# Row totals of two output norms by VectorE blocks of 32, and the second norm's factors as a row by HBM

## The chip, the cores and the metric

The kernel runs on one core of a Trainium2 chip. It computes one layer of an encoder block in float32. The metric is the device time of one execution in microseconds (us). Each engine (TensorE or PE for matmuls, VectorE or DVE, ScalarE or ACT, GpSimd or POOL, SyncE or SP for transfers) runs its own list of instructions in order, and semaphores tie the lists together.

## The reference

There are 256 tokens (S) of width 2048 (D). Cut to what matters here, with every norm an RMS norm (divide by the root of the mean square, multiply by a gain):

```python
h = rmsnorm(x, norm1_g)
q, k, v, u = split(h @ w_in)
a = rmsnorm(window_attention(q, k, v, sink), attn_out_g)   # 1536 wide: AW
f = rmsnorm(fourier_mix(u, w_fourier), fourier_out_g)      # 512 wide: FW
x = x + concatenate([a, f]) @ w_out
h = rmsnorm(x, norm2_g)
up = h @ w_up                                # gate (5504 wide) | value (5504 wide)
gate = depthwise_conv3(up_gate) + dw_b
x = x + (gelu(gate) * up_value) @ w_down
return rmsnorm(x, normf_g)
```

The change concerns three factors per token: those of the norms of `a` and of `f`, which are applied after the output projection, and that of the norm before `w_up` (the second norm), which is applied to the results of the up-projection.

## The kernel before, in words

**Products.** A float32 operand is split into a rounded half `hi` and the rest `lo`, and a product is three matmuls (hi·hi, lo·hi, hi·lo). The weights come from HBM as units of 128x2048 (1 MB, tile `raw`, three buffers), SP issuing the loads (L165). ACT writes `hi` (L181), DVE writes `lo` (L182); each has three buffers, so the split of a unit waits until PE is done with the unit three before it. The list of units, in order: 0 to 3 for u, 4 to 7 for v, 8 to 23 for the heads of k and q (32 matmuls each, L350), 24 to 39 for the output projection (24 matmuls each, L333 to L335), then one unit for each gate tile and each value tile of the up-projection (units 40, 41, 42, ... ; L350), mixed with the down-projection.

**The order of work.** It is written out by hand. `unit(i, work)` runs for each unit i: the list `before[i]`, the matmuls, the list `beside[i]`, then `step(i)`, which splits unit i + 2 and so issues the load of unit i + 5, then `behind[i]`. `at(when, i, f, ...)` puts f in one of these lists. In the up-projection `ff_step(n)` does the same for item n (item 0 is the first gate tile, item 1 the first value tile, and so on; item n is unit 40 + n here). `N_OUT` is 24.

**Sums for `a` and `f`.** The heads and Fourier groups are held with features on partitions and the 256 tokens along the free side. POOL adds up their squares into `sq_f` and `sq_a` (128 partitions x 256 tokens, L490). A token's total is thus a sum over partitions. `total` (L494) forms it on PE: two float32 matmuls with a column of `ones`, into a bank of `ps_tot`, at the head of unit 14 for `f` and of unit 30 for `a`. `total_scale` calls `rstd_of` (L274): DVE multiplies and adds EPS (L277), POOL raises to the power -0.5 (L280). The result `r_af[part]`, 128x2, holds tokens on partitions. `out_add` (L808) applies it on DVE when a result of the output projection leaves PSUM (L811); the first use for `f` is beside unit 29, for `a` behind unit 30.

**The second norm.** ACT sums the squares of the new x by rows (L285, `ssq2`). After the first two up-projection items have been multiplied in pieces (the pair: chunks 0 to 11 of item 0, `ff_step(0)`, the transposes of the last quarter of x on PE in `turn_x(3)`, chunks 0 to 11 of item 1, then chunks 12 to 15 of both), DVE reduces `ssq2` (L1225), `rstd_of` makes the factors with tokens on partitions, and `spread` (L289) turns them into a row that stands on all partitions: two diagonal matrices on DVE (L294), two float32 matmuls with `ones` on PE (L297), a copy on DVE out of PSUM into `r2b` (L300). Every up-projection result is then multiplied by `r2b` in `scaled_sum` (L920 to L925): ACT copies one half of the bank, DVE adds the other half (this frees the PSUM bank), DVE multiplies by `r2b`.

**A row by HBM.** `row_by_hbm` (L304) makes such a row without PE: a transfer from POOL's queue writes the 256 factors to HBM one by one (L307), a second reads them back as a row on all 128 partitions (L308). Before the change it is used once, for the first norm (`r1b`, behind unit 4).

**PSUM.** Up-projection results use the four banks of `mm` in turn, so item n needs the bank of item n - 4. `spread`, `total`, scores, values and transposes share the four banks of `dn`. `up_posts(n, ...)` puts `scaled_sum` beside item n + 1, the convolution of a gate tile beside and its GELU behind n + 2, and the product of gate and value beside n + 2.

Of the kernel before, what the change touches and what calls it, by code (L numbers as in the profile page):

```python
# [8 lines left out]
F32 = mybir.dt.float32  # L9
# [95 lines left out]
def block_kernel(  # L105
# [30 lines left out]
    def bank(pool, name):  # L136
        return pool.tile([P, 512], F32, tag=pool.name, name=name)
# [114 lines left out]

    ones = base.tile([P, P], F32, tag="ones", name="ones")
    nc.gpsimd.memset(ones, 1.0)
    half_pow = base.tile([P, 2], F32, tag="half_pow", name="half_pow")
    nc.gpsimd.memset(half_pow, -0.5)
    ident = base.tile([P, P], F32, tag="ident", name="ident")
    make_identity(nc, ident)
# [15 lines left out]
    def rstd_of(ssq, width, name, n=2, r=None):  # L274

        var = base.tile([P, n], F32, tag="var" + name, name="var" + name)
        nc.vector.tensor_scalar(var, ssq, 1.0 / width, EPS, ALU.mult, ALU.add)  # L277
        if r is None:
            r = base.tile([P, n], F32, tag="rstd" + name, name="rstd" + name)
        nc.gpsimd.tensor_tensor(r, var, half_pow[:, 0:n], ALU.pow)  # L280
        return r

    def row_ssq(parts, t, c, b, name):
# [1 line left out]
        nc.scalar.activation(  # L285
            junk, t[:, b, :], AF.Square, accum_out=parts[:, b, c : c + 1]
        )

    def spread(r, dst, name):  # L289

        t = wp.tile([P, 512], F32, tag="junk", name=f"diag{name}")
        dgs = [t[:, b * P : (b + 1) * P] for b in range(2)]
        for b, dg in enumerate(dgs):
            nc.vector.tensor_scalar(dg, ident, r[:, b : b + 1], None, ALU.mult)  # L294
        ps = bank(dn, "ps_spread" + name)
        for b in range(2):
            nc.tensor.matmul(  # L297
                ps[:, b * P : (b + 1) * P], ones, dgs[b], start=True, stop=True
            )
        nc.vector.tensor_copy(dst, ps[:, :S])  # L300

    rows = ctx.enter_context(tc.tile_pool(name="rows", bufs=1, space=bass.MemoryType.DRAM))

# [71 lines left out]
    def at(when, i, f, *a):  # L375
        when.setdefault(i, []).append((f, a))
# [112 lines left out]
        if not first:  # L489
            nc.gpsimd.tensor_tensor(sq, sq, one, ALU.add)  # L490

    sums, r_af = {}, {}

    def total(sq, part):  # L494
        ps = bank(dn, "ps_tot" + part)
        for b in range(2):
            nc.tensor.matmul(
                ps[:, b : b + 1], sq[:, b * P : (b + 1) * P], ones[:, 0:1],
                start=True, stop=True,
            )  # L500
        sums[part] = ps

    def total_scale(part, width):
        r_af[part] = rstd_of(sums.pop(part)[:, 0:2], width, part)


    held = {}
# [98 lines left out]
    def fourier_channels_steps():  # L606
        for g in range(NG):
            i = 8 + g
            at(before, i, fourier_channels, g)
            at(beside, i, fourier_channels_copy, g)  # L610
            at(behind, i, fourier_channels_join, g)
            at(beside, i + 1, fourier_channels_out, g)
        at(before, 14, total, sq_f, "f")
        at(beside, 14, total_scale, "f", FW)


    ps_v = [bank(mm, f"ps_v{b}") for b in range(2)]
# [206 lines left out]
    def turn_x(c):  # L824
        turn_x_out(c, turn_x_in(c))
# [47 lines left out]
                )  # L873
        hT2.append(t)

    at(before, N_OUT + 6, total, sq_a, "a")
    at(beside, N_OUT + 6, total_scale, "a", AW)
    ps_a = {}
    for n, (c, kq) in enumerate(OUT_ORDER):
        i = N_OUT + n  # L880
# [188 lines left out]
    def ff_step(n):  # L1069
        todo, later[:] = list(later), []  # L1070
        for f in todo:
            next(f, None)
        run(beside, n)
        split_item(n + 2)
        for f in todo:
            for _ in f:
                pass
        run(behind, n)

    def up_posts(n, kind, j, ps):  # L1080
        if kind == "gate":
            at(beside, n + 1, scaled_sum, ps, f"g{j}")
            at(beside, n + 2, gate_conv, j)
            at(behind, n + 2, gate_gelu, j)
        else:
            at(beside, n + 1, scaled_sum, ps, f"v{j}")
            at(beside, n + 2, val_mult, j)
            if j + 1 in [first + 2 * n for first, n in GROUPS]:
                g = group_of(j)[0]
                at(behind, n + 1, operand, g, "P1")  # L1090
                at(behind, n + 2, operand, g, "N4")
                at(behind, n + 3, operand_sums, g, 0)
# [120 lines left out]
    for q in range(2):  # L1213
        kind, j = items[q]
        ps = bank(mm, f"ps_{kind}{j}")
        pair.append((ps, *halves.pop(n_front + q)))
        still_weights(*pair[q][1:], ps, range(12))
        if q == 0:
            ff_step(0)
            turn_x(3)  # L1220
            hT[:] = hT2
    for ps, hi, lo in pair:
        still_weights(hi, lo, ps, range(12, NK))
    tot2 = base.tile([P, 2], F32, tag="tot2", name="tot2")
    nc.vector.tensor_reduce(tot2, ssq2, mybir.AxisListType.X, ALU.add)  # L1225
    spread(rstd_of(tot2, D, "2"), r2b, "2")
    ff_step(1)
    up_posts(1, *items[0], pair[0][0])
    up_posts(2, *items[1], pair[1][0])

    for n, it in enumerate(items):
        if n < 2:
# [205 lines left out]
```

## Time and profile before

| what | us |
|---|---|
| median of the runs shown | 938.24 (938.22 to 939.98, 3 runs) |
| the profiled execution's own time | 937.84 |
| its span, first to last instruction | 936.1 |
| PE busy in it | 926.8 |
| DVE busy | 767.0 |
| ACT busy | 541.3 |
| POOL busy | 62.2 |

The profile is one execution. The span leaves out what lies around the first and the last instruction, 1.74 us here. Matmuls are pipelined, so one of them overlaps the next; what a group of matmuls costs is the distance from the end of the group before it to its own end, and this is how the chain of waits counts. Times in the text are microseconds from the start of the span.

### The profile page before, as it was taken

To read this page: it belongs to the slowest core of one execution; us is meant where nothing else is said; L and a number is where in the kernel's file an instruction comes from. 1 tells how busy PE (TensorE), PEld (TensorE's weight loads), DVE (VectorE), ACT (ScalarE), POOL (GpSimd) and SP (SyncE) were. 2 spreads that over 40 slices of the span, in tenths; PEclk is the share of its full clock that TensorE was granted. 3 is DMA by queue.
4 is the path that set the end of the run, shared out by engine and by line. 5 is a ranking of instruction groups with operands and counts; after the bars stand their busy time and mean duration, and the time that the engine had idled before them with its cause. 6 is when DMAs were issued, how large, how long until landed. Compare 5 with 4: busy or idle time off the path is not lost.

```text
span 936.1 us, 12843 instructions
## 1 busy us (share of the span) xinstructions
PE 926.8 (99%) x5005; PEld 802.8 (86%) x5005; DVE 767.0 (82%) x958; ACT 541.3 (58%) x672; POOL 62.2 (7%) x80
## 2 busy tenths in 40 slices
PE   9999999999999999999999999999999999999996
PEld 7889998888888888888888888888888888888885
DVE  7668988577677887798877997878979789989986
ACT  6756777545464646566555665555655556655553
POOL 0101211100000000000000000000000000000002
PEclk9999999999999999999999999999999999999999
DMA  9965777567766568788797778777787968779652
GB/s 360 319 223 163 244 236 209 185 206 264 249 226 220 187 203 263 254 270 259 222 293 257 235 217 291 232 260 234 260 247 241 307 223 270 242 230 275 197 180 90
DMA packets 55149, 223.26 MB, mean 239 GB/s; under 512 B 21136, under 2 KB 25744, under 8 KB 31536
## 3 DMA queue, kind: packets, MB, share of 16 engines
q1 hardware_dynamic: 50544, 192.94, 57.1%
q0 software_dynamic: 4544, 29.49, 16.6%
q8 instruction: 39, 0.64, 0.3%
q14 instruction: 22, 0.18, 0.1%
HBM read 216.13 MB, written 6.29 MB: 238 GB/s over the span
## 4 chain that ended last, share of the span: by engine, by line
PE 98%; DVE 1%; DMA 0%; ACT 0%; issue 0%; DVEq 0%; POOLq 0%; POOL 0%; ACTq 0%
PE ps_val L350 25%; PE ps_gate L350 25%; PE ps_q L350 7%; PE ps_P L1149 3%; PE ps_P L1147 3%; PE ps_P L1148 3%; PE ps_N L1149 3%; PE ps_N L1147 3%; PE ps_N L1148 3%; PE ps_a L335 2%; PE ps_k L350 2%; PE ps_a L333 2%; PE ps_a L334 2%; PE ps_s L657 1%; PE ps_o L751 1%; PE ps_ff L333 1%
## 5 line engine op out<-in xcount | busy, mean ns | idle before, releaser
L182 DVE TENSOR_TENSOR lo<-raw,hi 128x2048 fp32r<-128x2048 f32 (+1 forms) x129 | 293.4, 2274 | 40.4 <-ACT hi L181 40.0
L181 ACT ACTIVATE hi<-raw 128x2048 fp32r<-128x2048 f32 (+1 forms) x129 | 245.5, 1903 | 36.9 <-PE ps_a L334 14.9
L350 PE MATMUL ps_val<-hU,hi 128*128 128x512 f32 x688 | 236.2, 390 | 0.0
L350 PE MATMUL ps_gate<-hU,hi 128*128 128x512 f32 x688 | 236.2, 390 | 0.0
L350 PE MATMUL ps_val<-hU,lo 128*128 128x256 f32 x688 | 190.3, 277 | 0.0
L350 PE MATMUL ps_gate<-hU,lo 128*128 128x256 f32 x688 | 190.3, 277 | 0.0
L350 PEld LDWEIGHTS ps_gate<-hU,hi 128*128 128x128 f32 x688 | 129.2, 188 | 26.8
L350 PEld LDWEIGHTS ps_val<-hU,hi 128*128 128x128 f32 x688 | 129.2, 188 | 26.8
L350 PEld LDWEIGHTS ps_gate<-hU,lo 128*128 128x128 f32 x688 | 129.3, 188 | 1.3
L350 PEld LDWEIGHTS ps_val<-hU,lo 128*128 128x128 f32 x688 | 129.3, 188 | 1.3
L922 ACT ACTIVATE ft_g<-ps_gate 128x256 f32<-128x256 f32 x43 | 16.5, 384 | 123.0 <-PE ps_gate L350 123.0
L922 ACT ACTIVATE ft_v<-ps_val 128x256 f32<-128x256 f32 x43 | 16.5, 384 | 91.7 <-PE ps_val L350 91.7
L350 PE MATMUL ps_q<-hT,hi 128*128 128x512 f32 x192 | 65.1, 392 | 0.0
L1147 PE MATMUL ps_P<-hi_P,op_P 128*128 128x512 f32 x144 | 56.1, 390 | 0.0
L1149 PE MATMUL ps_P<-lo_P,op_P 128*128 128x512 f32 x144 | 56.1, 390 | 0.0
L1148 PE MATMUL ps_P<-hi_P,op_P 128*128 128x512 f32 x144 | 56.1, 389 | 0.0
L350 PE MATMUL ps_q<-hT,lo 128*128 128x256 f32 x192 | 51.3, 277 | 0.0
L1039 DVE TENSOR_TENSOR lo_N<-sumw,hi_N 128x2048 fp32r<-128x2048 f32 (+1 forms) x20 | 41.5, 2076 | 9.4 <-ACT hi_N L1038 9.2
L1147 PE MATMUL ps_N<-hi_N,op_N 128*128 128x512 f32 x108 | 42.1, 390 | 0.0
L1148 PE MATMUL ps_N<-hi_N,op_N 128*128 128x512 f32 x108 | 42.1, 390 | 0.0
L1149 PE MATMUL ps_N<-lo_N,op_N 128*128 128x512 f32 x108 | 42.1, 390 | 0.0
L350 PEld LDWEIGHTS ps_q<-hT,hi 128*128 128x128 f32 x192 | 35.3, 188 | 6.5
(390 smaller groups left out, 1589.9 us busy)
## 6 DMA issues: line engine op xcount, KB each, us to landing
raw<-in_w_up SPq DMA_DIRECT2D x86, 1024.0 KB, 5.7
raw<-in_w_in SPq DMA_DIRECT2D x20, 1024.0 KB, 6.5
raw<-in_w_out SPq DMA_DIRECT2D x16, 1024.0 KB, 4.9
sumw<-in_w_down POOLq DMA_DIRECT2D x16, 1024.0 KB, 8.4
raw<-in_w_down_late SPq DMA_DIRECT2D x4, 1024.0 KB, 7.0
raw<-in_w_down_last SPq DMA_DIRECT2D x4, 768.0 KB, 4.1
turnp<-flip SPq DMA_DIRECT2D x40, 64.0 KB, 1.9
flop<-turnp SPq DMA_DIRECT2D x10, 256.0 KB, 3.5
```

Source lines behind the costliest of these rows:

```text
L181: nc.scalar.activation(hi[:, 0:n], raw[:, 0:n], AF.Copy)
L182: nc.vector.tensor_tensor(lo[:, 0:n], raw[:, 0:n], f32(hi[:, 0:n]), ALU.subtract)
L333: nc.tensor.matmul(ps, ah, wh, start=first and q == q0, stop=False)
L334: nc.tensor.matmul(ps, al, wh, start=False, stop=False)
L335: nc.tensor.matmul(ps, ah, wl, start=False, stop=last and q == q0 + len(kk) - 1)
L350: nc.tensor.matmul(ps[:, x], (hi, lo)[i][:, k * P : (k + 1) * P], hk(k)[:, x], start=n == 0 and k == 0, stop=n == len(order) - 1 and k == ...
L657: nc.tensor.matmul(ps[:, b * S : (b + 1) * S], qT[:, qo + b * P : qo + (b + 1) * P], kT[:, ko : ko + S], start=n == 0, stop=n == 2,)
L922: nc.scalar.activation(tmp, ps[:, S : 2 * S], AF.Copy)
L1039: nc.vector.tensor_tensor(lo, src, f32(hi), ALU.subtract)
L1147: nc.tensor.matmul(ps, o[:, 0, p, :], hi[:, s], start=first and p == 0, stop=False)
L1148: nc.tensor.matmul(ps, o[:, 1, p, :], hi[:, s], start=False, stop=False)
L1149: nc.tensor.matmul(ps, o[:, 0, p, :], lo[:, s], start=False, stop=last and p == n - 1)
```

## The change

`total` and `spread` go. `total_scale` now takes the sums of squares themselves and does all on DVE but the power: it transposes the 128x256 tile in blocks of 32x32, so that in each block the 32 partitions' values of a token lie side by side, adds them up (one reduction to 128x8), brings the three lower quarters of partitions next to the first (three copies of 32x8), adds the four, scales, lets POOL raise 32x8 to the power, and puts the result on 128x2 by four copies of 32x2. The calls move: for `f` from unit 14 to behind unit 25 (after the split of unit 27), for `a` from unit 30 to behind unit 29 (after the split of unit 31).

The factors of the second norm are formed right after `ff_step(0)`, ahead of `turn_x(3)`, and go to `r2b` by `row_by_hbm`. The work behind items 0 and 1 moves one item later (`up_posts` with 2 and 3 in place of 1 and 2).

```diff
-    half_pow = base.tile([P, 2], F32, tag="half_pow", name="half_pow")
+    half_pow = base.tile([P, 8], F32, tag="half_pow", name="half_pow")
...
-    def spread(r, dst, name):
...
-    def total(sq, part):
-        ps = bank(dn, "ps_tot" + part)
-        for b in range(2):
-            nc.tensor.matmul(
-                ps[:, b : b + 1], sq[:, b * P : (b + 1) * P], ones[:, 0:1],
-                start=True, stop=True,
-            )
-        sums[part] = ps
-
-    def total_scale(part, width):
-        r_af[part] = rstd_of(sums.pop(part)[:, 0:2], width, part)
+    def total_scale(sq, part, width):
+
+        t = ph.tile([P, S], F32, tag="tmp", name=f"turned_{part}", bufs=2)
+        nc.vector.transpose(t, sq)
+        w = ph.tile([P, S], F32, tag="add", name=f"sums_{part}", bufs=2)
+        q = w[:, 0:32].rearrange("p (q f) -> p q f", q=4)
+        nc.vector.tensor_reduce(
+            q[:, 0, :], t.rearrange("p (f i) -> p f i", f=8), mybir.AxisListType.X, ALU.add
+        )
+        for k in range(1, 4):
+            nc.vector.tensor_copy(q[0:32, k, :], q[32 * k : 32 * (k + 1), 0, :])
+        tot = base.tile([P, 8], F32, tag="var" + part, name="var" + part)[0:32]
+        r = w[0:32, 32:40]
+        nc.vector.tensor_reduce(
+            tot, q[0:32].rearrange("p q f -> p f q"), mybir.AxisListType.X, ALU.add
+        )
+        nc.vector.tensor_scalar(tot, tot, 1.0 / width, EPS, ALU.mult, ALU.add)
+        nc.gpsimd.tensor_tensor(r, tot, half_pow[0:32], ALU.pow)
+        d = r_af[part] = base.tile([P, 2], F32, tag="rstd" + part, name="rstd" + part)
+        by_block = r.rearrange("p (b f) -> p f b", b=2)
+        for k in range(4):
+            nc.vector.tensor_copy(d[32 * k : 32 * (k + 1)], by_block[:, k, :])
...
-        at(before, 14, total, sq_f, "f")
-        at(beside, 14, total_scale, "f", FW)
+        at(behind, N_OUT + 1, total_scale, sq_f, "f", FW)
...
-    at(before, N_OUT + 6, total, sq_a, "a")
-    at(beside, N_OUT + 6, total_scale, "a", AW)
+    at(behind, N_OUT + 5, total_scale, sq_a, "a", AW)
...
             ff_step(0)
+            tot2 = base.tile([P, 2], F32, tag="tot2", name="tot2")
+            nc.vector.tensor_reduce(tot2, ssq2, mybir.AxisListType.X, ALU.add)
+            row_by_hbm(rstd_of(tot2, D, "2"), r2b, "2")
             turn_x(3)
...
-    tot2 = base.tile([P, 2], F32, tag="tot2", name="tot2")
-    nc.vector.tensor_reduce(tot2, ssq2, mybir.AxisListType.X, ALU.add)
-    spread(rstd_of(tot2, D, "2"), r2b, "2")
     ff_step(1)
-    up_posts(1, *items[0], pair[0][0])
-    up_posts(2, *items[1], pair[1][0])
+    up_posts(2, *items[0], pair[0][0])
+    up_posts(3, *items[1], pair[1][0])
```

More of the change, by code (lines that the diff above doesn't have):

```diff
@@ L287, in row_ssq @@
         )
-    def spread(r, dst, name):
[L291 to L295, printed above, removed]
-        for b in range(2):
-            nc.tensor.matmul(
-                ps[:, b * P : (b + 1) * P], ones, dgs[b], start=True, stop=True
-            )
-        nc.vector.tensor_copy(dst, ps[:, :S])
     rows = ctx.enter_context(tc.tile_pool(name="rows", bufs=1, space=bass.MemoryType.DRAM))
@@ L490, in feature_out @@
             nc.gpsimd.tensor_tensor(sq, sq, one, ALU.add)
-    sums, r_af = {}, {}
-    def total(sq, part):
-        ps = bank(dn, "ps_tot" + part)
-        for b in range(2):
-            nc.tensor.matmul(
-                ps[:, b : b + 1], sq[:, b * P : (b + 1) * P], ones[:, 0:1],
-                start=True, stop=True,
-            )
-        sums[part] = ps
-    def total_scale(part, width):
-        r_af[part] = rstd_of(sums.pop(part)[:, 0:2], width, part)
+    r_af = {}
+    def total_scale(sq, part, width):
[19 more added lines that the diff above has]
+            nc.vector.tensor_copy(d[32 * k : 32 * (k + 1)], by_block[:, k, :])
     held = {}
```

## The prediction

> **What bounds the kernel now.** I read the page first (busy times, shares of the chain), then the chain in order of time around the three places that the change touches, then the transfers, and last the instructions of POOL, DVE and ACT around those places.
>
> ```profile
> PE 926.8 (99%) x5005; PEld 802.8 (86%) x5005; DVE 767.0 (82%) x958; ACT 541.3 (58%) x672; POOL 62.2 (7%) x80
> PE 98%; DVE 1%; DMA 0%; ACT 0%; issue 0%; DVEq 0%; POOLq 0%; POOL 0%; ACTq 0%
> ```
>
> PE is busy for 926.8 us of a span of 936.1, and 98% of the chain that ended last is PE itself. So a microsecond taken out of PE's list is a microsecond of the kernel, wherever it stands, and work on DVE, ACT, POOL or the queues costs nothing as long as it does not make PE wait. The whole question is then how much leaves PE, and whether one of the new detours is long enough to stop it.
>
> The chain shows the three pieces of PE work that go. Columns: start, length, what, number of instructions.
>
> ```profile
> 84.70 5.48 PE ps_q L350 x32
> 90.18 0.34 PE ps_totf L497 x4
> 90.51 5.58 PE ps_q L350 x32
> 183.17 0.23 PE ps_ff L333
> 194.11 0.34 PE ps_tota L497 x4
> 194.45 0.34 PE ps_ff L333
> 195.94 0.23 PE ps_ff L333
> 260.81 0.44 PE ps_spread L297 x4
> 261.25 5.45 PE ps_gate L350 x32
> 277.58 5.44 PE ps_val L350 x32
> ```
>
> **Part 1, PE's own work.** The reader sees 0.34 us for the total of `f`, 0.34 for that of `a`, 0.44 for `spread`, and that the work behind each is a little longer than its like: 5.58 against 5.48 us for a unit of 32 matmuls (0.10), 0.34 against 0.23 for the first matmul behind the total of `a` (0.11), 5.45 against 5.44 behind `spread` (0.01). Removed: 0.34 + 0.10 + 0.34 + 0.11 + 0.44 + 0.01 = 1.34 us. If the small excesses have another cause, it is 0.34 + 0.34 + 0.44 = 1.12. I take 1.34, because the excess stands directly behind the removed group in two cases of three.
>
> **Part 2, the totals on DVE.** These are the rows of DVE around the new places of the two calls.
>
> ```profile
> 157.93 0.71 DVE L314 STREAM_TRANSPOSE flip<-sc 128x512 f32<-128x512 f32 x1
> 165.25 2.29 DVE L182 TENSOR_TENSOR lo<-raw,hi 128x2048 fp32r<-128x2048 f32 x1
> 172.34 2.29 DVE L182 TENSOR_TENSOR lo<-raw,hi 128x2048 fp32r<-128x2048 f32 x1 [0.48 <-ACT hi L181]
> 190.43 2.29 DVE L182 TENSOR_TENSOR lo<-raw,hi 128x2048 fp32r<-128x2048 f32 x1 [0.44 <-ACT hi L181]
> 195.86 2.29 DVE L182 TENSOR_TENSOR lo<-raw,hi 128x2048 fp32r<-128x2048 f32 x1 [1.22 <-ACT hi L181]
> ```
>
> And these are POOL's powers and its two transfers for the row of the first norm, then DVE's and ACT's rows around the second norm.
>
> ```profile
> 35.73 2.71 POOL L280 TENSOR_TENSOR rstd<-var,half_pow 128x2 f32<-128x2 f32 x1 [34.25 <-DVE var L277]
> 38.77 0.93 POOL L307 DMA_DIRECT2D row<-rstd  x1 [0.32 <-POOL rstd L280]
> 49.48 0.59 POOL L308 DMA_DIRECT2D r1b<-row  x1 [9.78 <-DMA row<-rstd]
> 257.37 0.69 POOL L280 TENSOR_TENSOR rstd<-var,half_pow 128x2 f32<-128x2 f32 x1 [61.95 <-DVE var L277]
> ```
>
> ```profile
> 250.76 2.29 DVE L182 TENSOR_TENSOR lo<-raw,hi 128x2048 fp32r<-128x2048 f32 x1 [0.18 <-ACT hi L181]
> 254.09 0.48 DVE L270 SCALAR_TENSOR_TENSOR hU<-ps_x,vec,hU 128x256 fp32r<-128x256 f32 x1 [1.04 <-ACT hU L269]
> 256.94 0.15 DVE L1225 TENSOR_REDUCE tot<-ssq 128x2 f32<-128x8 f32 x1
> 257.12 0.17 DVE L277 TENSOR_SCALAR var<-tot 128x2 f32<-128x2 f32 x1
> 263.83 0.42 DVE L924 TENSOR_TENSOR fa_g<-ps_gate,ft_g 128x256 f32<-128x256 f32 x1
> 264.28 0.43 DVE L925 TENSOR_TENSOR fa_g<-fa_g,r2b 128x256 f32<-128x256 f32 x1
> 264.62 2.29 DVE L182 TENSOR_TENSOR lo<-raw,hi 128x2048 fp32r<-128x2048 f32 x1
> 266.82 0.48 DVE L933 SCALAR_TENSOR_TENSOR cv<-fa_g,vec,cv 128x255 f32<-128x255 f32 x1
> 267.74 0.41 DVE L924 TENSOR_TENSOR fa_v<-ps_val,ft_v 128x256 f32<-128x256 f32 x1
> ```
>
> ```profile
> 251.91 0.19 ACT L285 ACTIVATION_READ_ACCUMULATOR junkb<-xs 128x1 f32 x1
> ```
>
> One call of the new `total_scale` costs DVE a transpose of half the size of the one shown, between 0.35 and 0.71 us, say 0.45; a reduction over 256 elements, for which no row exists, taken like the 256-element operations at 0.42 to 0.48; nine small operations like the 0.15 and 0.17 of the reduction and scaling, 9 x 0.16 = 1.4; and the wait for POOL's power, 0.69 and some 0.1 of handing over. That is 3.1 us, an estimate from these rows. The power has been seen at 0.69 and at 2.71; the 2.71 lies over a run of DVE's split, and here DVE waits idle, so I take 0.69; with 2.71 the call takes 5.1. In front of `f` stands the split of unit 27 (165.25, ends 167.54), so the call ends at about 170.6. Even if all 3.1 or 5.1 us went into the next split (172.34, ends 174.63), unit 28 would be ready at 177.7 or 179.7, and PE opens it at 183.17. For `a` the call runs from 192.72 to about 195.8, in a gap in which DVE waits anyway until 195.86; with 5.1 us the next split, of unit 32, ends at 200.1 and PE opens unit 32 two units of some 5.4 behind the one at 194.45, at 205.3. Cost 0 at the value taken and at the upper end; the cover is a lead of 5 us or more, and what a call took beyond it would be PE's. The factor for `a` is first used behind unit 30, after that split, as before.
>
> **Part 3, the row by HBM.** Reduction and scaling move from 256.94 to the end of the split at 250.76, that is 253.05 (ACT's last sum of squares has ended at 252.10); they take 0.18 + 0.17 of the 1.04 us in which DVE then waits for ACT, so the transposed x is not later. POOL's list is empty there. Its power starts 0.25 behind the scaling, as at 257.37, at 253.48 and ends at 254.17; the write of the 256 factors is issued 0.33 later, 254.50. For the two transfers there is one precedent, and two neighbours (size, median to landing):
>
> ```profile
> turnp<-flip SPq DMA_DIRECT2D x40, 64.0 KB, 1.9
> gfb<-in_normf_g POOLq DMA_DIRECT2D x1, 1024.0 KB, 4.5
> r1b<-row POOLq DMA_DIRECT2D x1, 128.0 KB, 6.9
> row<-rstd POOLq DMA_DIRECT2D x1, 1.0 KB, 10.1
> ```
>
> At least, a write to HBM lands in 1.9 us and a broadcast in 4.5; the precedent says 10.1 and 6.9. I take the precedent, since it is the same pair of instructions: row landed at 264.6, read issued 0.6 later (48.87 to 49.48 in the precedent) at 265.2, `r2b` landed at X = 272.1. The lower end is 254.50 + 1.9 + 0.6 + 4.5 = 261.5.
>
> Who waits for X? DVE, in the first multiplication by `r2b`, which now stands beside item 3, behind the splits of items 3 and 4; DVE would be there near 265.5, so it stands still for up to 6.6 us. Behind it on DVE, by the rows at 264.28 to 267.74: the rest of that multiplication 0.34, addition and multiplication for item 2 0.45 + 0.34, the split of item 5 2.20, the convolution 0.92, and then the addition that frees the PSUM bank of item 1, 0.41. Together X + 4.66 = 276.8. PE needs that bank for item 5, which begins at 277.58 now and 0.45 earlier without `spread`, 277.13 (the 0.89 of the two totals moves everything here alike). So there are 0.35 us to spare, and a landing later than 272.5 makes PE wait by as much as it is later. The next in line, the split of item 6, would be ready about 4.2 us later, at X + 8.9 = 281.0, against 283.02 - 0.45 = 282.57 of PE. The bank of item 0, needed for item 4, is freed by an addition that stands ahead of the wait. Cost taken: 0.
>
> The Trainium skill, "DMA: Bandwidth & Descriptors", section "Anatomy of one DMA — SWDGE (gpsimd) path", puts such a transfer at about 2.0 us fixed plus its bytes over the bandwidth, most of the fixed part being the receipt of the write, and calls the delay long where the target is HBM. By that estimate `r2b` would land at about 259 and DVE would never wait; the rows here, 10.1 for 1 KB and 6.9 for 128 KB, disagree by a factor of 3 to 5, and I go by them.
>
> What else goes on the queues: the removed DVE work (two diagonals, one copy out of PSUM) frees DVE for its splits near 258 to 262; SP's list is not touched, but the small writes share the transfer engines with the weight loads. The windows of the precedent and of the new place (last columns: granted clock, share of the transfer engines, GB/s):
>
> ```profile
> 38.00:49.00 11.00, 11.00 (x62) 9.55 (x61) 7.57 (x10) 7.72 (x10) 1.38 (x2) 1.00 0.75 143
> 49.00:57.00 8.00, 8.00 (x43) 6.87 (x42) 4.44 (x4) 4.69 (x5) 0.59 (x1) 1.00 0.90 321
> 254.00:265.00 11.00, 11.00 (x67) 9.79 (x67) 6.24 (x13) 5.62 (x8) 0.69 (x1) 1.00 0.31 103
> 265.00:273.00 8.00, 8.00 (x50) 7.08 (x48) 7.86 (x12) 5.76 (x9) 0.00 (x0) 1.00 0.98 385
> ```
>
> The write falls into a quieter stretch than its precedent (0.31 against 0.75), so 10.1 should rather be too long; the read falls into a slightly busier one (0.98 against 0.90). Weight loads there are needed only some 8 us after they land, so a pause of the write's length costs 0.
>
> **Sum.** 1.34 off PE, 0 added. The profiled execution's own time 937.84 gives 936.5; it lies 0.4 below the median of the runs shown, so against the median 938.24 - 1.34 = 936.9, 0.14% faster.
>
> **Rivals.**
>
> *A, the bank makes PE wait a little.* X later than 272.5. If the read behind the weight loads takes 8.4 instead of 6.9, X is 273.6, PE waits 1.1 and the result is 938.0. For it: 0.98 of the engines busy. Against it: the quiet stretch under the write.
>
> A variant comes from the power. The Trainium skill, "SBUF — State Buffer", section "SBUF: two separate sides", says that POOL is shut out for a whole DVE instruction that reads two SBUF operands. The 2.71 us beside 0.69 agree with it. For the sum, a power of 2.71 means X = 274.1, a wait of 1.6 and 938.5; against it stands that DVE's next instruction, at 254.09, reads from PSUM and starts as the power ends.
>
> *B, slower.* The same place, one mechanism: the read of the row stands behind the loads that SP has issued just before and takes as long as the write did, 10.1 or more. X = 275.3 at 10.1 gives a wait of 2.8 and 939.7; from X = 272.5 + 1.34 + 1.88 = 275.7 on the kernel is slower by over 0.2%. At 11.5 it is X = 276.7, a wait of 4.2, 941.1. Against it: its precedent took 6.9 under 0.90.
>
> *C, the change does less.* If the excess behind the removed groups stays, 1.12 go and the result is 937.1.
>
> *D, more goes.* The matmuls that go last longer singly than in the chain:
>
> ```profile
> L497 PE MATMUL ps_tota<-ones,sq_a x4: 165/250/250, 193.9 to 194.2; 128*128 128x1 f32 x4
> ```
>
> Four of 0.25 us in each total, and as much for `spread`, are 3.0 us; if none of it overlapped, 935.2. Against it: the distances in the chain are 0.34, and PE shows no gap around them.
>
> **How the numbers follow.** About 0.2% (1.9 us) is what a measurement of this kernel can tell from no change. The forecast (no wait, 1.34 off) has 0.60, C 0.07, A with its variant 0.15; these are within 0.2%, together 0.82, of which I move 0.03 to faster for scatter of the median, as the profiled execution was 0.4 below it. B has 0.07, and 0.02 go to a wait that I have not seen: slower 0.09. D has 0.09, so faster 0.12, same 0.79. The likeliest case gives 936.9, alone within 936.4 to 937.4. The range 936.2 to 938.4 takes in A and C up to the power's 2.71 and the scatter below; it leaves out B and most of D.
>
> **What would show it right or wrong.** Right: no `ps_tot` and `ps_spread` in the chain, PE without a gap from 4.5 us on, its end about 1.3 earlier. Part 2: two calls of about 3 us on DVE behind the splits of units 27 and 31, the power at 0.7. Part 3: the write issued near 253.6 and landed near 263.7 (0.89 earlier than above), `r2b` near 271.2, DVE idle before its first multiplication by `r2b` for some 5 to 6 us, item 5 on PE without a wait. Wrong: a gap on PE at item 5 or 6, or a span that does not follow PE's shorter list.

## The result and the profile after

| | us |
|---|---|
| before, median of 22 executions | 938.08 (937.62 to 939.98) |
| after, median of 22 executions | 936.77 (936.44 to 952.23) |
| ratio, with its 95% interval | 0.9987 (0.9981 to 0.9993) |
| predicted | 936.9 (936.2 to 938.4) |

The change takes off 938.08 - 936.77 = 1.31 us by the medians, where 1.34 were forecast; the interval of the ratio leaves out 1, and the gain is smaller than the 0.2% that the prediction took as the least that can be told from no change. One execution took some 15 us longer than the rest; the ratio is formed without it, and by the mean of all 22 the gain is only 0.57 us (938.13 against 937.56). The profiled execution of the changed kernel was that long one, 952.23 us, while the other 21 lay between 936.44 and 937.54; the same kernel was therefore run again (first experiment, 937.21 us in its profiled execution), and that profile is read here. The long one is read after it, because it shows something of its own.

From the page of the repeated run: the span, the busy times, and the chain's shares by engine.

```profile
span 935.4 us, 12841 instructions
PE 925.5 (99%) x4993; PEld 801.9 (86%) x4993; DVE 770.7 (82%) x975; ACT 541.4 (58%) x672; POOL 63.7 (7%) x82
PE 98%; DVE 1%; DMA 0%; ACT 0%; issue 0%; DVEq 0%; POOLq 0%; POOL 0%; ACTq 0%
```

Twelve instructions have left PE (5005 to 4993), 17 have come to DVE and 2 to POOL, and PE still carries 98% of the chain. The chain around the three places (start, length, what, number):

```profile
84.83 10.94 PE ps_q L337 x64
...
193.78 0.23 PE ps_ff L320
...
258.62 1.36 PE ps_val L337 x8
259.99 5.44 PE ps_gate L337 x32
...
276.31 5.44 PE ps_val L337 x32
```

No group for totals or `spread` is left: two units of heads follow each other in 10.94 us where before, with the total of `f` between them, they took 5.48 + 0.34 + 5.58 = 11.40; the first matmul of unit 30 takes 0.23, not 0.34 behind another 0.34; the first whole gate item follows the pair's pieces directly. From the start of that pair of units to the start of the gate item were 261.25 - 84.70 = 176.55 us and are now 259.99 - 84.83 = 175.16, which is 1.39 less.

DVE around the new place of the total of `f`, and POOL's powers and transfers:

```profile
164.93 2.29 DVE L182 TENSOR_TENSOR lo<-raw,hi 128x2048 fp32r<-128x2048 f32 x1
167.14 0.44 DVE L484 STREAM_TRANSPOSE turned_f<-sq_f 128x256 f32<-128x256 f32 x1
167.61 0.42 DVE L487 TENSOR_REDUCE sums_f<-turned_f 128x8 f32<-128x256 f32 x1
168.07 0.51 DVE L491 COPY sums_f<-sums_f 32x8 f32<-32x8 f32 x3
...
170.79 1.22 DVE L502 COPY rstdf<-sums_f 32x2 f32<-32x2 f32 x4 [1.79 <-POOL sums_f L498]
...
173.75 2.28 DVE L182 TENSOR_TENSOR lo<-raw,hi 128x2048 fp32r<-128x2048 f32 x1
```

```profile
169.09 1.68 POOL L498 TENSOR_TENSOR sums_f<-varf,half_pow 32x8 f32<-32x8 f32 x1 [1.81 <-DVE varf L497]
194.25 1.64 POOL L498 TENSOR_TENSOR sums_a<-vara,half_pow 32x8 f32<-32x8 f32 x1 [9.60 <-DVE vara L497]
252.66 0.72 POOL L280 TENSOR_TENSOR rstd<-var,half_pow 128x2 f32<-128x2 f32 x1 [56.77 <-DVE var L277]
253.68 0.79 POOL L294 DMA_DIRECT2D row<-rstd  x1 [0.29 <-POOL rstd L280]
263.76 0.57 POOL L295 DMA_DIRECT2D r2b<-row  x1 [9.29 <-issue]
```

The call for `f` holds DVE from 167.14 to 172.01, 4.9 us (between the rows shown stand two short ones, the adding of the four and the scaling); in 1.79 of them DVE waits for the power, which takes 1.68 on 32x8. The row of the second norm is issued at 253.68 and read at 263.76. DVE behind it, and all the waits of PE in the whole execution (line, releaser: us in total, times, longest):

```profile
264.91 0.42 DVE L920 TENSOR_TENSOR fa_g<-ps_gate,ft_g 128x256 f32<-128x256 f32 x1
271.27 0.43 DVE L921 TENSOR_TENSOR fa_g<-fa_g,r2b 128x256 f32<-128x256 f32 x1 [5.95 <-DMA r2b<-row]
271.62 0.42 DVE L920 TENSOR_TENSOR fa_g<-ps_gate,ft_g 128x256 f32<-128x256 f32 x1
...
272.41 2.28 DVE L182 TENSOR_TENSOR lo<-raw,hi 128x2048 fp32r<-128x2048 f32 x1
...
275.53 0.42 DVE L920 TENSOR_TENSOR fa_v<-ps_val,ft_v 128x256 f32<-128x256 f32 x1
```

```profile
PE ps_warm L262 <- POOL ones L254: 1.0, 1, 1.0
PE ps_u L399 <- ACT hT L269: 0.2, 1, 0.2
```

DVE stands still for 5.95 us until `r2b` has landed (271.2), and PE does not notice: both of its waits belong to the first microseconds. PE's first matmul with `lo` of item 5 starts at 276.37, and that split ends at about 274.6: 1.7 us to spare.

**The execution of 952.23 us.** Its chain from the write of the row on:

```profile
255.03 10.44 DMA row<-rstd
...
266.54 6.22 DMA r2b<-row
...
273.99 2.30 DVE lo L182
276.29 0.04 issue
276.33 5.50 PE ps_val L337 x31
281.83 5.75 PE ps_gate L337 x32
287.58 5.60 PE ps_val L337 x32
```

Here the row is issued 1.35 us later (255.03 against 253.68), `r2b` lands at 272.76, and the split of item 5 ends at 276.29, after PE has asked for it. PE itself stands 0.45 us earlier in this execution (its first matmul of item 5 starts at 275.69, in the repeated run at 276.14), so against PE the row lands 2.0 us later, and the 1.7 to spare are gone. The lateness comes from elsewhere: DVE and ACT ahead of it waited for a transfer that turns x by way of HBM. ACT's row at that place, here and in the repeated run:

```profile
243.89 1.71 ACT L866 ACTIVATE hU<-flopx,vec 128x256 fp32r<-128x256 f32 x4 [5.31 <-DMA flopx<-turnx]
```

```profile
242.54 1.71 ACT L866 ACTIVATE hU<-flopx,vec 128x256 fp32r<-128x256 f32 x4 [3.51 <-DMA flopx<-turnx]
```

PE itself waits for 0.25 us only (its row in the long execution):

```profile
276.33 0.39 PE L337 MATMUL ps_val<-hU,lo 128*128 128x256 f32 x1 [0.25 <-DVE lo L182]
```

What costs 15 us is what follows, and it does not start at that wait. Behind it the pairs of matmuls (a `hi` one over 512 columns, a `lo` one over 256) come every 340 ns again after the first of them, as they do in the repeated run. It starts at item 6. The split of item 6 ends at 281.89, just as PE comes to it (the DVE row, and PE's first two matmuls of item 6):

```profile
279.61 2.28 DVE L182 TENSOR_TENSOR lo<-raw,hi 128x2048 fp32r<-128x2048 f32 x1
```

```profile
281.67 0.39 PE L337 MATMUL ps_gate<-hU,hi 128*128 128x512 f32 x1
281.95 0.39 PE L337 MATMUL ps_gate<-hU,lo 128*128 128x256 f32 x1
```

The `lo` matmul starts 0.28 us behind the `hi` one and lasts 0.39; in the repeated run it starts 0.23 behind and lasts 0.28. From there on the pairs come every 350 ns without any wait between them, with a granted clock of 1.00 in the windows from 282 to 400 and 600 to 720 us, and this goes on until about 860 us. An item of 32 matmuls takes 5.60 us in place of 5.44: the 75 items of that stretch take 420.1 us where they take 408.0 in the repeated run, and the 65 groups of the down-projection between them 160.8 where they take 157.8. That is 15.1 us, all of the difference.

### The profile page after: what moved, and what is told of

It reads as the page before. It is cut to its first block, busy times and chain, and to the rows that moved or that the text cites. A ratio compares the mean times of both kernels' runs of the same rounds, so it can differ in the third digit from the quotient of the medians.

```text
span 950.4 us, 12841 instructions
## 1 busy us (share of the span) xinstructions
PE 940.5 (99%) x4993; PEld 807.6 (85%) x4993; DVE 770.8 (81%) x975; ACT 541.4 (57%) x672; POOL 63.7 (7%) x82
## 4 chain that ended last, share of the span: by engine, by line
PE 93%; DMA 3%; DVE 2%; issue 1%; ACT 0%; SPq 0%; DVEq 0%; POOL 0%; POOLq 0%; ACTq 0%
PE ps_val L337 24%; PE ps_gate L337 24%; PE ps_q L337 7%; PE ps_P L1145 4%; PE ps_P L1144 3%; PE ps_P L1143 3%; PE ps_N L1145 3%; PE ps_N L1144 3%; PE ps_N L1143 3%; PE ps_k L337 2%; PE ps_a L322 2%; PE ps_a L320 2%; PE ps_a L321 2%; DMA row<-rstd 1%; PE ps_s L654 1%; PE ps_o L748 1%
## 5 line engine op out<-in xcount | busy, mean ns | idle before, releaser
L337 PE MATMUL ps_gate<-hU,hi 128*128 128x512 f32 x688 | 242.1, 394 | 0.0
L337 PE MATMUL ps_val<-hU,hi 128*128 128x512 f32 x688 | 242.0, 394 | 0.0
L337 PE MATMUL ps_val<-hU,lo 128*128 128x256 f32 x688 | 192.7, 280 | 0.3 <-DVE lo L182 0.3
L337 PE MATMUL ps_gate<-hU,lo 128*128 128x256 f32 x688 | 192.7, 280 | 0.0
```

What stands on the lines that cost most here:

```text
L337: nc.tensor.matmul(ps[:, x], (hi, lo)[i][:, k * P : (k + 1) * P], hk(k)[:, x], start=n == 0 and k == 0, stop=n == len(order) - 1 and k == ...
```

## The experiments

The theory behind the prediction: the gain is the work that left PE and nothing else, and the row by HBM is hidden as long as it lands in time. The rivals: the gain of one part is eaten by the other; the long executions come with the row's transfers; or a wait of PE can bring them, whatever made PE wait. Ratios are against runs of the kernel before on the same chip.

**The changed kernel again.** No edit.

> The changed kernel itself once more, for a second profile. Theory (PE's list decides, the row comes in time): 1.3 us under the kernel before, near 936.8, PE without a gap, the row's read landed at 271 to 273 and the split of item 5 finished before PE asks for it at about 276.0. Rival (the row is late on the chip as in the profile shown): PE waits some tenths of a us at item 5 or 6, and behind that wait the pairs of hi and lo matmuls follow each other every 350 ns in place of 340, which costs up to 14 us more: near 951.

937.15 us (936.94 to 938.68, 10 executions), before 938.27: 0.9992 (0.9983 to 1.0001). Its profile is the one above. The gain on this chip is 1.12 us, within the interval of the first; its own interval just takes in no change.

**The totals by DVE alone.** The row of the second norm stays with `spread` on PE, ahead of `ff_step(1)`, and the posts stay unshifted.

```diff
-            row_by_hbm(rstd_of(tot2, D, "2"), r2b, "2")
...
+    spread(rstd_of(tot2, D, "2"), r2b, "2")
     ff_step(1)
-    up_posts(2, *items[0], pair[0][0])
-    up_posts(3, *items[1], pair[1][0])
+    up_posts(1, *items[0], pair[0][0])
+    up_posts(2, *items[1], pair[1][0])
```

> Only the totals by DVE; the second norm's factors by the diagonal matrices and PE as before, and the work behind items 0 and 1 where it was. Theory: what leaves PE is what is gained, 0.44 + 0.45 = 0.89 us: ratio 0.9990 to the kernel before. Rival (the totals' matmuls lay in the shadow of other PE work, or DVE's calls cost what they bring): ratio 1.0000, the whole gain in the row by HBM.

937.02 us (936.90 to 937.55, 11 executions): 0.9988 (0.9980 to 0.9997). By medians this part alone takes off 1.25 us, as much as the whole change on the same chip (1.12): the scatter of the medians is as large as what the second part adds.

**The row by HBM alone.** The totals stay on PE.

```diff
-        at(behind, N_OUT + 1, total_scale, sq_f, "f", FW)
+        at(before, 14, total, sq_f, "f")
+        at(beside, 14, total_scale, "f", FW)
-    at(behind, N_OUT + 5, total_scale, sq_a, "a", AW)
+    at(before, N_OUT + 6, total, sq_a, "a")
+    at(beside, N_OUT + 6, total_scale, "a", AW)
```

> Only the row by HBM with the work behind items 0 and 1 one item later; the totals on PE as before. Theory: 0.45 us off: ratio 0.9995. Rival (the row's detour is the gain or the loss): either over 1 us off, ratio below 0.9990, or a wait of PE at item 5 that eats it, ratio 1.0000 or more.

937.86 us (937.50 to 954.24, 11 executions): 0.9998 (0.9989 to 1.0007). The median fell by 0.41, `spread` being 0.45 by the prediction, but the interval takes in no change: that this part gains is read from PE's chain, not from the times. One of the eleven took 954.24, and it was the profiled one: there the same transfer that turns x came late, `r2b` landed at 275.01, PE waited 1.4 us for the split of item 5, and here too the pairs went back to 340 ns behind that wait and turned to 350 only at item 6, whose split ended at 284.15 (first `lo` matmul at 284.20); the items behind it took 5.60 us.

**The posts not shifted.** The changed kernel, but the work behind items 0 and 1 stands where it stood before, so that DVE needs `r2b` one item earlier.

```diff
-    up_posts(2, *items[0], pair[0][0])
-    up_posts(3, *items[1], pair[1][0])
+    up_posts(1, *items[0], pair[0][0])
+    up_posts(2, *items[1], pair[1][0])
```

> The changed kernel with the work behind items 0 and 1 left where it was before the change (beside items 2 and 3), so that DVE meets the first multiplication by the row ahead of the split of item 4. Theory: DVE stands still until the row lands, at about 271.2 to 272.8; the split of item 4 ends 2.6 later, at 273.8 to 275.4, and PE asks for it at about 270.5: PE waits 3.3 to 4.9 and the time is 936.8 + 3.3 to 4.9, that is 940.1 to 941.7, ratio 1.002 to 1.004. Rival 1 (the row lands much earlier than the prediction took): no wait, 936.8. Rival 2 (a wait of PE also changes the pace of the matmuls behind it): up to 14 us more, 950 to 956.

954.90, 956.02, 939.19 and 956.25 us. The chain of the first:

```profile
270.79 2.30 DVE lo L182
273.08 0.04 issue
273.13 5.63 PE ps_gate L337 x31
278.76 5.60 PE ps_val L337 x32
```

PE waits 2.56 us for the split of item 4, and the pairs come every 350 ns from there on. The execution of 939.19 lies 2.0 us above the changed kernel, which would be a wait of about that length without the pace; it has no profile. In the profiled one the pace comes on top, and the two of about 956 us have its length. So the shift of the posts is a needed part of the change: without it a row that lands at 270.4 stops PE.

**One hop more.** The row is copied once more in HBM before it is read.

```diff
+        for hop in range(1 if name == "2" else 0):
+            more = rows.tile([2, P], F32, tag=f"row{name}{hop}", name=f"row{name}{hop}")
+            nc.gpsimd.dma_start(more, row)
+            row = more
```

> The changed kernel with one more station for the row: it is copied once within HBM between the write and the read, which makes it later by 2.5 to 5 us and changes nothing else. Theory (PE waits by as much as the row is late beyond about 272.3): the row lands at 273.7 to 276, PE waits 1.4 to 3.7 us at item 5, 938.3 to 940.6. Rival (a wait of PE there also turns the pace of the pairs of matmuls from 340 to 350 ns up to about 855 us): up to 14 us more, 952 to 955.

938.93 us (937.24 to 941.62, 10 executions), before 938.40: 1.0012 (1.0002 to 1.0021). In the profiled one, 937.99 us, `r2b` landed at 273.34, about 2 us later than without the hop, and PE waited 0.7 us at item 5:

```profile
276.91 5.64 PE ps_val L341 x31
282.55 5.48 PE ps_gate L341 x32
```

The pairs behind that wait come every 350 ns, but only to the head of item 6, whose split was ready in time (it ended at 282.48, and the first `lo` matmul starts at 282.63); from its third pair on they come every 340, and the later items take 5.44. That execution is 0.8 us above the profiled one of the repeated run (937.21), about the length of the wait, and still 0.4 below the kernel before; by the median of the ten the gain has become a loss. So the cover was not large. None of these ten took more than 941.62 us. The three longest (940.6 to 941.6) have a mean granted clock of 0.995 or 0.996, where the kernel before has 0.997 or 0.998; the next experiment shows where that can come from.

**A wait without the row.** The kernel before, with DVE made busy for some 6 us beside one gate item, 7 in one kernel (about 335 us) and 26 in the other (about 620 us). Added work on DVE only; the edit for gate item 7 is shown.

```diff
+    def busy():
+        t = wp.tile([P, 512], F32, tag="junk", name="busy")
+        nc.vector.memset(t, 0.0)
+        for _ in range(8):
+            nc.vector.tensor_tensor(t, t, t, ALU.add)
+
+    at(beside, items.index(("gate", 7)), busy)
```

> The kernel before the change with some 5 us of idle additions on DVE (one memset and eight additions on 128x512 of a spare tile, beside the gate item 7, at about 332 us): nothing else is touched, so PE must wait about 2.5 to 3 us once for a split. Theory A (a wait costs its own length): 938.2 + 2.5 to 3 = 940.7 to 941.2. Theory B (a wait turns the pace of the pairs to 350 ns for what is left of the up-projection, 0.0245 us lost per us up to about 855): 12.8 more, 953.5 to 954.

> The same idle additions beside the gate item 26, at about 617 us. Theory A: 940.7 to 941.2 again, independent of the place. Theory B: 0.0245 x (855 - 620) = 5.8 more than A, 946.5 to 947.

Early: 958.57, 957.08, 943.99 and 943.53 us. Late: 941.96, 947.41, 942.91 and 942.95. The chain of the 958.57:

```profile
340.78 2.21 DVE lo L182
342.99 0.04 issue
343.03 8.03 PE ps_val L350 x31
...
352.44 5.60 PE ps_gate L350 x32
```

Nothing is changed at the second norm, and no transfer is moved: PE waits 3.8 us, and the items behind it take 5.60 us. The item right behind the wait takes 8.03, because the granted clock has fallen to half (last columns: granted clock, share of the transfer engines, GB/s):

```profile
343.00:347.00 4.00, 3.97 (x12) 3.43 (x13) 3.04 (x6) 3.19 (x4) 0.00 (x0) 0.50 0.68 258
```

It fell during the wait and is back at 1.00 by 348.5; by the length of that item the half clock costs some 2.6 us. So this wait has two prices beside its own length: the half clock, for some 5 us, and the pace of 350 ns, for hundreds. The wait of 3.0 us in the profiled late one (941.96 us) shows neither: the clock stays at 1.00 and the items behind it take 5.44.

The expectations had a wait of 2.5 to 3 us; in the profiled ones it was 3.8 and 3.0. The two shorter early ones lie 5.1 and 5.6 us over 938.40, which a wait of about 3.8 and part of such a stretch of half clock would make up; their mean granted clock, 0.995 and 0.996, fits that, but they have no profile. Of the late ones one lies 4.5 us above the middle of the other three, which lie 3.6 to 4.6 over 938.40; its mean clock is 0.998, so it is not the clock, and theory B had 5.8 for it. This agrees with the third rival as far as it goes: the pace can turn without any change to the row. It also shows that a wait does not always turn it.

**The row in blocks.** The factors are turned by DVE into four rows of 32 on partitions, and SP writes them to HBM as eight runs of 128 bytes; the read is as before. `wide` and `turned` are two blocks of 32 columns of the tile of ones, which nothing else reads by then.

```diff
-            row_by_hbm(rstd_of(tot2, D, "2"), r2b, "2")
+            rstd_of(tot2, D, "2", r=wide[:, 0:2])
             turn_x(3)
+            nc.vector.transpose(turned, wide)
+            row = rows.tile([2, 4, 32], F32, tag="row2", name="row2")
+            for k in range(4):
+                nc.sync.dma_start(row[:, k, :], turned[32 * k : 32 * k + 2, :])
+            nc.gpsimd.dma_start(r2b, row.rearrange("b k i -> (b k i)").partition_broadcast(P))
```

> The changed kernel with the row of the second norm's factors brought to HBM in another way: DVE turns the factors in blocks of 32 behind the transposes of x, and SP writes 8 runs of 128 bytes in place of POOL's 256 single values; the read stays. Theory (the 10 us of the write come from its single values): the write lands in 2 to 4 us, the row at about 257 + 3 + 0.6 + 7 = 264 to 268 in place of 271.2, DVE's stand ahead of its first multiplication by the row shrinks from 6 us to 0 to 3, and as PE's list is the same, the time stays at 936.8 to 937.2, without the wait of PE that the changed kernel shows in some executions. Rival (the write takes its time whatever its form): the row lands at 274 or later, PE waits 2 us and more at item 5.

952.75 us (952.12 to 952.81, 5 executions): 1.0156 (1.0142 to 1.0170). `r2b` landed at 265.07, 6 us earlier, and PE waited for nothing; and yet every item was slow, with a length that is neither of the two seen so far:

```profile
262.37 5.55 PE ps_gate L337 x32
```

This kernel differs in one more way. The tile of 32 bytes for the second norm's factors is gone, so all tiles behind it in SBUF, the weights' `hi`, `lo` and `raw` among them, stand 32 bytes lower (in the built programs `hi` of item 0 lies at 110336 instead of 110368). Three runs took that apart.

**The same, with the addresses kept; and the addresses alone.** The first is the row in blocks again, but keeps that tile and copies it into the block (one more DVE copy of 128x2). The second is the changed kernel with only the tile dropped, the third the changed kernel with another 32 bytes ahead.

```diff
-            rstd_of(tot2, D, "2", r=wide[:, 0:2])
+            r2 = rstd_of(tot2, D, "2")
             turn_x(3)
+            nc.vector.tensor_copy(wide[:, 0:2], r2)
```

```diff
-            row_by_hbm(rstd_of(tot2, D, "2"), r2b, "2")
+            row_by_hbm(rstd_of(tot2, D, "2", r=ones[:, 0:2]), r2b, "2")
```

```diff
+    spare = base.tile([P, 2], F32, tag="spare", name="spare")
+    nc.gpsimd.memset(spare, 0.0)
```

> The row in blocks again (eight runs of 128 bytes from SP), but the 32-byte tile of the second norm's factors is kept (the factors are copied out of it into the block that is transposed), so that every tile stands at the address that it has in the changed kernel. Theory (the 347 ns per pair of the first version came from the weight tiles having moved by 32 bytes): pairs at 340 ns throughout, r2b lands near 265 instead of 271, no wait on PE at item 5, no execution tipped into the 350 ns pace; median 936.8 to 937.4, ratio 0.9985 to 0.9992, as the changed kernel, and the highest of the runs below 939. Rival (the eight small writes on SP's queue, or the read early, slow the pairs): 347 ns again and 952 to 953, ratio 1.0155.

> The changed kernel with one difference: the second norm's two factors per token are written into the first two columns of the tile of ones (which is used no more by then) instead of a tile of 32 bytes of their own, so that the weight tiles and all else behind it in SBUF stand 32 bytes lower. Same instructions on every engine. Address theory: pairs of the up-projection near 347 ns from the first one on, r2b still landing near 271, 951 to 953, ratio 1.0155. Rival (addresses do not matter): 936.8 to 937.4, ratio 0.9990.

> The changed kernel with an additional tile of 32 bytes ahead, set to zero once on POOL in the first microseconds, so that the weight tiles stand 32 bytes higher. Address theory: the time moves by more than the 1 us scatter, up or down, with the pairs' pace (the first move gave 347 against 340 ns, some 15 us; I know of nothing that says whether this one is better or worse, and take 945 to 955 as the likelier). Rival (addresses do not matter): 936.8 to 937.4, ratio 0.9990.

| kernel | us (range, executions) | ratio |
|---|---|---|
| row in blocks, addresses kept | 937.07 (936.38 to 938.07, 11) | 0.9986 (0.9977 to 0.9995) |
| changed kernel, 32 bytes lower | 952.96 (952.22 to 953.89, 4) | 1.0155 (1.0140 to 1.0169) |
| changed kernel, 32 bytes higher | 936.89 (936.79 to 937.70, 10) | 0.9985 (0.9976 to 0.9994) |

The slow items of the first version in blocks were due to the addresses. From the chain of the kernel 32 bytes lower: two units of heads take 11.12 us against 10.94, long before the row exists, and the items of the up-projection take 5.55. (In its profiled execution PE also waits 0.9 us for a split at item 5; the first version in blocks is as slow without any wait.)

```profile
86.07 11.12 PE ps_q L337 x64
...
291.41 5.55 PE ps_val L337 x32
```

Of the third my leaning (945 to 955) was wrong: 32 bytes higher is as good as the place it had. With the addresses kept, the row in blocks does what it was made for (POOL and DVE at the place where DVE stood for 5.95 us):

```profile
259.73 0.62 POOL L1226 DMA_DIRECT2D r2b<-row  x1 [6.09 <-issue]
```

```profile
264.79 0.42 DVE L921 TENSOR_TENSOR fa_g<-ps_gate,ft_g 128x256 f32<-128x256 f32 x1
265.24 0.42 DVE L922 TENSOR_TENSOR fa_g<-fa_g,r2b 128x256 f32<-128x256 f32 x1
```

DVE goes from the addition to the multiplication without a stand; `r2b` landed 3.5 us after its issue, at 263.2, 8 us earlier than by single values. It gains no time, since nothing waited, but the split of item 5 now ends at 269.8, more than 6 us ahead of PE, where it was 1.7. All eleven executions lie below 938.1; against 1 long one in 22 of the changed kernel, that is too few to call it shown that the long ones are gone.

**The unshifted posts, 32 bytes higher.** Both edits as above: does the slow pace behind a wait go away in another layout, too?

> The posts of items 0 and 1 unshifted (the edit that made PE wait 2.6 us at item 4, after which three of four executions took about 955 us), in the layout 32 bytes higher. Theory (the pace that a wait can tip into depends, like the pace from the start in the layout 32 bytes lower, on where the tiles stand): the wait alone remains, 938.5 to 940 in all executions. Rival (a wait can tip the pace in any layout): about 955 in most executions, with pairs at 350 ns behind the wait.

941.12 us (938.63 to 958.63, 10 executions): three took 954.0 to 958.6, the others 938.6 to 943.8. The profiled one, 939.90 us, has the wait and, from the second pair behind it on, the normal pace:

```profile
PE ps_gate L339 <- DVE lo L182: 1.7, 1, 1.7
```

So the theory fails: an execution some 15 us longer can follow in this layout as well, though in fewer than the "most" of the rival. None of the three has a profile; that their pace is that of 350 ns is inferred from their times. Whether it does so less often there (3 of 10 against 3 of 4) these numbers can't say.

## Why the prediction was right, step by step

**Part 1, right.** The terms were 0.34 + 0.10 for the total of `f`, 0.34 + 0.11 for that of `a`, 0.44 + 0.01 for `spread`, together 1.34. The distance on PE shrank by 1.39, and the medians by 1.31 and 1.12. The two terms that were doubtful, the excess behind the totals, went too: 11.40 became 10.94 for the two units of heads. That the first median came within 0.03 of the forecast is luck, since the two medians of the same comparison differ by 0.19. By parts, the totals alone gave 1.25 (0.89 forecast, interval of the ratio 0.3 to 1.9 us) and the row alone 0.41 (0.45, with an interval that takes in 0). The 1.12 of rival C and the 3.0 of rival D are told apart as far as D goes: a gain of 3 us lies outside every interval. C against the forecast is 0.22 us, less than the medians scatter; only the distances on the chain (10.94 for the two units, 0.23 now for the first matmul of unit 30) speak for 1.34.

**Part 2, no cost, but the call was mis-sized.** 3.1 us were forecast; the call for `f` took 4.9 and that for `a`, by the same rows, 4.3. The power on 32x8 takes 1.68 and 1.64, not the 0.69 that I took from one on 128x2, and the four last copies 1.22 in one of the calls (0.67 in the other), not 0.64. The upper end, 5.1, held, and so did the cover: the next split (173.75) ended near 176.0, before PE's opening of unit 28 near 183. The call for `a` ran over the gap that it was given (the next split starts as it ends, at 196.6), but that split too was done at 198.9, before PE opened unit 32 near 204.7.

**Part 3, the landing hit by errors that cancel.** Forecast for the axis of the changed kernel: issued 253.6, landed 263.7, `r2b` 271.2, an idle DVE for 5 to 6 us. Measured: 253.68, 262.7, 271.18, and 5.95. The write took 9.0 where its precedent took 10.1; from its landing to the issue of the read went 1.06, not 0.6; the read took 7.4, not 6.9. The Trainium skill, "DMA: Bandwidth & Descriptors", section "Anatomy of one DMA — SWDGE (gpsimd) path", by whose 2 us plus bytes the row would have been there at about 259 by the prediction's estimate, is contradicted for the write of single values (9.0 us here); the read comes nearer to it behind the eight runs (3.5 us in the row in blocks with the addresses kept). The variant of rival A did not come: POOL's power took 0.72, not 2.71.

*The step of part 3 that failed* is "PE needs that bank for item 5". It is not the tight spot. In the execution of 952.23 us item 5 was begun before the addition that frees item 1's bank had run on DVE, so it used another bank; that the four banks are taken strictly in turn was true of the kernel before and was assumed for the changed one. In the built program of the changed kernel item 5 has the bank of item 2, whose addition stands ahead of that of item 1 on DVE since the posts are shifted (271.62 and 275.53 in the repeated run), and the bank of item 1 goes to item 6. What PE waits for is `lo` of item 5, 3.4 us behind X (3.33 by the prediction's own rows); the margin is 1.7 us, not the 0.35 that I had. The place (item 5) was right by chance. The next in line, the split of item 6, was named rightly, and it is there that both profiled long executions with the posts shifted turn (this kernel and the row alone).

*"a pause of the write's length costs 0"* held for the time, and the pause exists. Median times from issue to landing of the weight loads between 250 and 275 us, before, then repeated run, then row in blocks with the addresses kept:

```profile
raw<-in_w_up SPq DMA_DIRECT2D x4, 1024.0 KB, 5.2
```

```profile
raw<-in_w_up SPq DMA_DIRECT2D x4, 1024.0 KB, 7.6
```

```profile
raw<-in_w_up SPq DMA_DIRECT2D x4, 1024.0 KB, 5.0
```

So a weight load takes 2.4 us longer in the repeated run. In all eight profiles of kernels that write this row as 256 single values the median is 5.4 to 9.8 us; in the six others, the two with eight runs of 128 bytes among them, it is 4.9 to 5.2. How the write holds up the loads is not shown.

**The rivals.** A and B counted a wait of PE at its length. The extra hop shows that price in its profiled execution (a landing 2 us later, a wait of 0.7 us, a time 0.8 above that of the changed kernel). But in 1 of 22 executions of the change, where X came 2.0 us later against PE because x was turned late, PE waited 0.25 us for the split of item 5 and met that of item 6 as it ended, and the pace that turned there cost 15. That is the sign of being wrong that the prediction names, a gap on PE at item 5. Its price was in none of the cases, and no row of before could have given it: its PE never waits behind the first 5 us.

## What to carry to other kernels

Where PE carries nearly the whole chain, the gain of moving small matmuls off it can be read from the distances in the chain, to a few tenths of a microsecond, and the matmuls' own durations (0.25 us each here) would have said more than twice as much (3.0 against 1.34). What then decides is the margin of the detour, which is to be taken from the split or load that PE asks for next, counted from the late transfer, rather than from a rule about the banks. A tile added or dropped moves every tile behind it: keep the addresses in an experiment, or the experiment measures them instead.

## What the runs showed that was not expected

*Addresses.* 32 bytes lower for the weight tiles and all else behind one small tile cost 15 to 16 us in every execution (medians 952.96 and 952.75 against 936.89 to 937.15), 32 bytes higher cost nothing; an up-projection item took 5.55 us against 5.44. Why is open; which of the moved tiles does it was not tried.

*A wait can turn the pace.* Leaving out the layout 32 bytes lower, seven profiled executions have a wait of PE for a split in the up-projection. In four of them the pairs of matmuls then came every 350 ns instead of 340 for hundreds of us: at once behind waits of 2.56 and 3.8 us, and in two only at the next item, whose split ended just as PE came to it. In the other three (waits of 0.7, 3.0 and 1.7 us) the pace was back at 340 within an item or so. Counted by times of more than 950 us, it was 1 of 22 with the change, 1 of 11 with the row alone, 3 of 4 and 3 of 10 with the posts unshifted, 2 of 4 behind the early added work, 0 of 10 behind the extra hop. Of 97 executions of the kernel before, none took more than 940 us. In all four the slow pace ends at the same item, which starts between 862.8 and 868.9 us, behind the first matmuls of another form since the output projection (L320 to L322, L333 to L335 in the kernel before). The granted clock is not the cause: it is 1.00 along the slow stretch. What is out of step then is not shown by these traces. The added work shows that the row is not needed for it; that a late split is what turns the pace is the reading that fits all four, not a proof.

*A wait can be followed by half the clock.* During the wait of 3.8 us the granted clock fell to 0.50, and it stayed there for some 5 us of the work behind it, until about 348.3; with the waits of 0.25 to 3.0 us in the other profiled executions it stayed at 1.00. One profile shows it.

*Single values are dear in two ways.* 1 KB as 256 values of 4 bytes takes 8.8 to 11.3 us to HBM over all profiles, and the weight loads beside it take longer; as eight runs of 128 bytes, issued between 256.49 and 257.69, it was in HBM in time for a read issued at 259.73.
